# Ten of sixteen expert pairs: rows stored in DRAM and fetched per token, in place of the scatter matmul

## The chip, the cores and the metric

The kernel runs on one core of a Trainium2 chip. The time is device microseconds (us) of one launch. A NeuronCore has five engines with their own instruction queues: TensorE (PE, matmuls; its weight loads are listed apart as PEld), VectorE (DVE), ScalarE (ACT), GpSimd (POOL) and SyncE (SP, which here issues nearly all DMAs). They meet only through semaphores. Data lie in DRAM, in SBUF (128 partitions) and in PSUM, the matmul's output banks.

## The reference

Two layers of a streaming encoder on 512 tokens of width 1024 in float32. Each layer mixes tokens, attends to a memory, and ends with a mixture of experts, which is what the change touches:

```
for l in range(DEPTH):                    # 2 layers
    ...mixers, cross-attention, layer norms...
    g_p, g_idx   = top_1(softmax(t @ w_group))              # 4 groups
    e_p, e_idx   = top_2(softmax(logits of the 8 experts of that group))
    gate[t, e]   = g_p * e_p / sum(e_p)                     # 2 of 32 experts a token
    for e in range(32):
        h   = silu(t @ w_gate[e]) * (t @ w_up[e])           # 1024 -> 256
        out = out + (h @ w_down[e]) * gate[:, e]            # 256 -> 1024
    x = layer_norm(ALPHA * x + out)
```

An expert's weights are 1024x512 (gate and up) and 256x1024 (down) floats, 3.1 MB; 32 experts are 100.7 MB a layer.

## The kernel before, in words

Each expert has 64 slots; a token chosen by more than 64 goes to an overflow loop that runs after the experts. A token's slot number is 64 e + its rank in expert e, kept for its two experts in `s` (tokens on partitions, four tiles of 128 tokens). Two experts with neighbouring numbers form a pair of 128 slots, so a layer has 16 pairs; pairs 2q and 2q+1 share a block of 256 slots whose tokens are gathered by one-hot matmuls (`gather`, L1313) into a transposed tile `XX`.

The loop of `moe` (L1421) makes one run per pair p. On PE a run is, in this order: `down` of pair p-1 (h @ w_down, L1383, two halves of 512 columns), `up` of pair p (L1360, 8 steps of contraction for 2 experts), then four gather chunks for the next block (L1320) with `turn` of pair p (two transposes of h, L1373) and, between them, the scatter of pair p-1. `scatter` (L1497) multiplies a one-hot matrix `ohT` (128 slots by 512 tokens) with the pair's output `y`, for four token tiles and two halves: 8 results, each of 2 matmuls, because `y` is held as a rounded part and a rest (`e_y`, L1385 on ACT and L1386 on DVE, both with the gate `ws` as factor). Each result is added to the residual `x` on DVE (L1506). `onehot_rows` (L1476) makes `ohT` and `ws` with five DVE passes over 512 columns a pair. The last two blocks' runs (14 and 15) gather nothing. After run 15 `down` and the scatter of pair 15 follow, with sums for the layer norm (L1508).

Weights come in tiles of 128x1024 floats (512 KB): 8 for gate and up and 4 for down, 12 a pair, 192 a layer. `moe_raw` (L369) hands out buffers for them from a ring of 22: five `e2`, four `e1`, three each of `raw`, `whi`, `wlo`, and one 4-fold buffer `T16` (printed T). SP issues the loads in the ring's order, and waits in its queue until a buffer's last reader is done. A load of SP also waits until the one that used its completion semaphore is done; there are eight of these, so about eight loads are under way at a time. In the last run of layer 0 `fill_ahead` (L1391) loads two tiles of the memory (`in_memT`) for the next layer into one `whi` and one `wlo`, which ACT and DVE then split into a rounded part and a rest (L350, L351).

The order on each queue is that of a scheduler in the tile framework, which places instructions by their own due times; `issue_after` (`chain`, L279) keeps the PE runs of the loop in the order above.

Of the kernel before, what the change touches and what calls it, by code (L numbers as in the profile page):

```python
# [8 lines left out]
F32 = mybir.dt.float32  # L9
# [12 lines left out]
P = 128  # L22
# [186 lines left out]
class K:  # L209
    def __init__(self, ctx, tc, a):  # L210
        self.tc, self.nc, self.a = tc, tc.nc, a
        self.n = 0
        self.n_e1, self.n_e2, self.n_raw = 8, 5, 0
        self.n_rw, self.n_hi, self.n_lo, self.n_fw = 3, 3, 3, 3
        self.fills = [dict(f) for f in FILLS]
        self.mark, self.marks = None, False
        self.n_gap, self.n_u1, self.n_u2, self.n_qk = 1, 12, 8, 2
        self.paged = {}
# [150 lines left out]
    def moe_raw(self):  # L369
# [970 lines left out]

    def experts(self, Xs, gu, dn, ws, page, dpage=None):

# [34 lines left out]
        def down(hf, run):  # L1377
            if hf == 0:
                y.extend(self.t([P, D], "e_y", 2, F32R, self.mp) for _ in range(2))
            po, c = self.bank(self.pj), slice(hf * 512, (hf + 1) * 512)  # L1380
            for k in range(2):
                for i in range(n):
                    run.append(nc.tensor.matmul(po[CAP * i:CAP * i + CAP, :], st["hT"][:, k, CAP * i:CAP * i + CAP],  # L1383
                                                st["w"][k][i][:, c], start=k == 0, stop=k == 1))
            nc.scalar.activation(y[0][0:R, c], po[0:R, :], AF.Copy, scale=ws)  # L1385
            nc.vector.scalar_tensor_tensor(y[1][0:R, c], po[0:R, :], ws, y[0][0:R, c], op0=OP.mult, op1=OP.subtract)  # L1386
# [22 lines left out]
    def moe(self, l, r, X, x, following):  # L1409
# [9 lines left out]
        last = NE // 2 - 1  # L1419
        self.marks, before = True, None  # L1420
        for p in range(NE // 2):  # L1421
            q, pr = p // 2, p % 2
            e = 2 * p
            if p == last:
                self.fill = iter(())
                if following and self.n_gap:
                    self.fill_ahead(following)
            up, act, turn, down, y = self.experts(
                XX[:, q % 2, :, 128 * pr:128 * pr + 128], [a["gu"][l * NE + e + i] for i in range(2)],
                [a["dn"][l * NE + e + i] for i in range(2)], ws[:, p:p + 1], self.moe_raw,  # L1430
                None if p < last else lambda: self.t([P, 1024], "e2", self.n_e2, pool=self.e2))

# [205 lines left out]
    def layer(self, l, x_src, xT):  # L1638
# [89 lines left out]
```

## Time and profile before

| | |
|---|---|
| median of 3 runs | 1618.11 us (1613.19 to 1619.2) |
| the profiled execution | 1623.95 us, its span 1622.1 us |
| PE, DVE, ACT, POOL busy | 96%, 66%, 36%, 2% of the span |
| mean granted TensorE clock | 0.978 of full speed |
| DMA in all | 303.04 MB, 186 GB/s over the span |
| experts of layer 0: first `up` to the last scatter | 497.88 to 792.2 us |
| experts of layer 1: first `up` to the last scatter | 1289.04 to 1581.6 us |

Busy time of PE is that of modelled, overlapping matmuls, so a busy PE need not be at its peak. DMA share is the mean busy share of the 16 DMA engines. A row of the waits says which engine and line waited and what came last before it went on. The two layers' expert stages are alike: the second starts 791.2 us after the first, and takes 1.7 us less from its first `up` to its last scatter.

### The profile page before, as it was taken

What the parts mean: (1) busy time and instruction counts of PE and PEld (TensorE: products, weight loads), DVE (VectorE), ACT (ScalarE), POOL (GpSimd) and SP (SyncE); (2) the same over time, 40 slices, a digit from 0 to 9 for tenths busy, and PEclk for the clock granted to TensorE, in tenths of its full rate; (3) what the DMA queues carried; (4) which work ended last, traced back from release to release, by engine and by line L of the source; (5) the groups of instructions that cost most, each with busy time, mean ns of one, the idle gap of its engine ahead of it and who ended that gap; (6) DMA issues with size and microseconds to landing.
All of it is one profiled execution on the core that took longest, in us unless ns stands there. A gap on an engine that the chain in (4) does not pass through costs nothing. (4 is left out here: it accounts for less than half of the span.)

```text
span 1622.1 us, 25953 instructions
## 1 busy us (share of the span) xinstructions
PE 1555.0 (96%) x10270; PEld 1151.0 (71%) x10270; DVE 1067.8 (66%) x2352; ACT 575.9 (36%) x1026; POOL 32.5 (2%) x44
## 2 busy tenths in 40 slices
PE   7999999999999999999889999999999999999994
PEld 6988876898896555555579888669889855555542
DVE  6768678675568954445767857777655798545454
ACT  6434346324323222222463442552342332222212
POOL 0000000010000000000000000001000000000100
PEclk9999899999999999999999989999999999999997
DMA  6432220522437999996543332033224599899861
GB/s 218 149 119 80 79 72 20 177 68 82 155 121 268 381 341 343 342 352 247 212 152 106 104 98 93 6 122 94 92 86 153 184 351 373 326 339 346 333 238 53
DMA packets 90656, 303.04 MB, mean 187 GB/s; under 512 B 10404, under 2 KB 10916, under 8 KB 90404
## 3 DMA queue, kind: packets, MB, share of 16 engines
q1 hardware_dynamic: 90532, 301.36, 52.7%
q8 instruction: 81, 1.33, 0.3%
q14 instruction: 43, 0.35, 0.1%
HBM read 292.93 MB, written 8.39 MB: 186 GB/s over the span
## 5 line engine op out<-in xcount | busy, mean ns | idle before, releaser
L386 PE MATMUL pj<-whi,T 128*128 128x256 f32 x640 | 183.4, 287 | 4.5 <-ACT T L846 2.8
L1506 DVE TENSOR_TENSOR e<-e,sm 128x512 f32<-128x512 f32 x240 | 153.2, 683 | 51.1 <-PE sm L1502 50.7
L388 PE MATMUL pj<-wlo,T 128*128 128x256 f32 x640 | 182.9, 286 | 3.8 <-DVE wlo L351 3.8
L387 PE MATMUL pj<-whi,T 128*128 128x256 f32 x640 | 182.4, 285 | 0.0
L386 PE MATMUL pj<-T,whi 128*128 128x512 f32 (+1 forms) x368 | 135.3, 368 | 5.9 <-ACT T L350 5.6
L1502 PE MATMUL sm<-e_y,e_oT 128*128 128x512 f32 x512 | 139.3, 397 | 1.3 <-ACT e_y L1385 0.8
L351 DVE TENSOR_TENSOR wlo<-raw,whi 128x1024 fp32r<-128x1024 f32 x86 | 104.7, 1221 | 51.2 <-ACT whi L350 50.7
L387 PE MATMUL pj<-T,wlo 128*128 128x512 f32 (+1 forms) x368 | 135.9, 370 | 2.3 <-DVE wlo L351 2.3
L1320 PEld LDWEIGHTS sm<-oh,T 128*128 128x128 f32 x896 | 117.5, 188 | 25.7 <-issue 17.8
L388 PE MATMUL pj<-T,whi 128*128 128x512 f32 (+1 forms) x368 | 135.0, 368 | 0.0
L1320 PE MATMUL sm<-oh,T 128*128 128x256 f32 x896 | 129.6, 287 | 0.0
L386 PEld LDWEIGHTS pj<-whi,T 128*128 128x128 f32 x640 | 123.9, 194 | 5.8 <-ACT T L846 3.0
L388 PEld LDWEIGHTS pj<-wlo,T 128*128 128x128 f32 x640 | 123.8, 194 | 5.3 <-DVE wlo L351 5.1
L350 ACT CAST whi<-raw 128x1024 fp32r<-128x1024 f32 x86 | 89.8, 1048 | 105.2 <-PE pj L387 57.4
L387 PEld LDWEIGHTS pj<-whi,T 128*128 128x128 f32 x640 | 123.9, 194 | 0.2
L1360 PE MATMUL pj<-e,T 128*64 128x512 f32 x448 | 110.2, 593 | 0.0
L1310 ACT ACTIVATE T<-sm,vec 128x256 f32<-128x256 f32 x116 | 65.3, 566 | 105.1 <-PE sm L1320 105.1
L1502 PEld LDWEIGHTS sm<-e_y,e_oT 128*128 128x128 f32 x512 | 88.1, 188 | 20.4 <-ACT e_y L1385 3.3
L1368 DVE TENSOR_TENSOR e_sl<-e_sl,pj 128x256 f32<-128x256 f32 x32 | 13.5, 421 | 132.7 <-ACT e_sl L1367 132.6
L1385 ACT ACTIVATE e_y<-pj,rws 128x512 fp32r<-128x512 f32 x64 | 43.8, 687 | 118.6 <-PE pj L1383 106.7
L1360 PEld LDWEIGHTS pj<-e,T 128*64 128x64 f32 x448 | 35.1, 137 | 69.9 <-issue 67.7
L386 PEld LDWEIGHTS pj<-T,whi 128*128 128x128 f32 x368 | 70.5, 192 | 17.5 <-ACT T L350 6.4
(483 smaller groups left out, 3200.0 us busy)
## 6 DMA issues: line engine op xcount, KB each, us to landing
e<-in_gu SPq DMA_DIRECT2D x112, 512.0 KB, 9.3
raw<-in_pieces SPq DMA_DIRECT2D x94, 512.0 KB, 3.6
e<-in_dn SPq DMA_DIRECT2D x60, 512.0 KB, 7.6
T<-in_gu SPq DMA_DIRECT2D x44, 512.0 KB, 7.4
wlo<-in_gu SPq DMA_DIRECT2D x36, 512.0 KB, 8.9
whi<-in_gu SPq DMA_DIRECT2D x34, 512.0 KB, 8.8
raw<-in_gu SPq DMA_DIRECT2D x34, 512.0 KB, 8.5
fw<-in_pieces SPq DMA_DIRECT2D x60, 256.0 KB, 3.0
```

Of the source, the lines that this page charges most:

```text
L350: self.nc.scalar.copy(hi, src)
L351: self.nc.vector.tensor_tensor(lo, src, hi, op=OP.subtract)
L386: mm(ps, a[0], b[0], start=first, stop=False)
L387: mm(ps, a[1], b[0], start=False, stop=False)
L388: return mm(ps, a[0], b[1], start=False, stop=last)
L1310: self.nc.scalar.activation(Xs[:, f, :], ps, AF.Identity, scale=v[:, VC_LG + f:VC_LG + f + 1], bias=v[:, VC_LB + f:VC_LB + f + 1])
L1320: run.append(nc.tensor.matmul(ps, X[i][t][:, f * P:(f + 1) * P], oh[:, t, :], start=i + t == 0, stop=i + t == NT))
L1360: run.append(nc.tensor.matmul(st["h"][CAP * i:CAP * i + CAP, :], Xs[:, k, i * CAP:(i + 1) * CAP], st["w"][i][:, (k % 2) * 512:(k % 2 + 1) ...
L1368: nc.vector.tensor_tensor(sl[0:R], sl[0:R], st["h"][0:R, DE:], op=OP.mult)
L1385: nc.scalar.activation(y[0][0:R, c], po[0:R, :], AF.Copy, scale=ws)
L1502: m = nc.tensor.matmul(ps, ohT[:, t * P:(t + 1) * P], y[i][0:n, c], start=i == 0, stop=i == 1)
L1506: nc.vector.tensor_tensor(x[t][:, c], x[t][:, c], ps, op=OP.add)
```

## The change

Pairs 0 to 9 no longer have a one-hot matrix, a scatter or additions. Their `down` copies each PSUM half unscaled into one float32 tile `e_y` (half 0 by ACT, half 1 by DVE), and ACT issues a DMA that stores its 128 rows at slots 128 p to 128 p + 127 of a DRAM tensor `yd`, one for each layer. At the start of run 12 `stored_rows` is recorded: for each of a token's two experts and each token tile, GpSimd clears a buffer of the ring, then issues an indirect DMA that fetches, by slot number (`si`, an integer copy of `s`), each token's row of `yd`; slots of 1280 and above are out of bounds and fetch nothing. DVE multiplies the fetched tile by the token's gate and adds it to `x`. That is 8 tiles of 128x1024 a layer. Pairs 10 to 15 keep the scatter. Since the 8 fetched tiles come from the ring, the pairs after them use other buffers than before; in the last pair the `T16` part of the ring is skipped.

```
--- before.py
+++ after.py
@@ -215,6 +215,7 @@
         self.fills = [dict(f) for f in FILLS]
         self.mark, self.marks = None, False
         self.n_gap, self.n_u1, self.n_u2, self.n_qk = 1, 12, 8, 2
+        self.n_st = 10
         self.paged = {}
         pool = lambda name, bufs=1, **k: ctx.enter_context(tc.tile_pool(name=name, bufs=bufs, **k))
         self.cp = pool("cp")
@@ -372,6 +373,9 @@
         ring += [("raw", self.n_rw, self.wp)] * self.n_rw + [("whi", self.n_hi, self.wp)] * self.n_hi
         ring += [("wlo", self.n_lo, self.wp)] * self.n_lo
         i = self.n_raw % (len(ring) + 4)
+        if i == len(ring) and self.tail:
+            self.n_raw += 4
+            i = 0
         self.n_raw += 1
         if i < len(ring):
             tag, n, pool = ring[i]
@@ -1338,7 +1342,7 @@
                 nc.scalar.activation(Xs[:, f, :], ps[:, k * CAP:(k + 1) * CAP], AF.Identity,
                                      scale=v[:, VC_LG + f:VC_LG + f + 1], bias=v[:, VC_LB + f:VC_LB + f + 1])
 
-    def experts(self, Xs, gu, dn, ws, page, dpage=None):
+    def experts(self, Xs, gu, dn, ws, page, dpage=None, dst=None):
 
 
         nc = self.nc
@@ -1376,12 +1380,17 @@
 
         def down(hf, run):
             if hf == 0:
-                y.extend(self.t([P, D], "e_y", 2, F32R, self.mp) for _ in range(2))
+                y.extend(self.t([P, D], "e_y", 2, F32R if dst is None else F32, self.mp) for _ in range(2 if dst is None else 1))
             po, c = self.bank(self.pj), slice(hf * 512, (hf + 1) * 512)
             for k in range(2):
                 for i in range(n):
                     run.append(nc.tensor.matmul(po[CAP * i:CAP * i + CAP, :], st["hT"][:, k, CAP * i:CAP * i + CAP],
                                                 st["w"][k][i][:, c], start=k == 0, stop=k == 1))
+            if dst is not None:
+                self.copy(y[0][:, c], po, "ad"[hf])
+                if hf:
+                    nc.scalar.dma_start(dst, y[0])
+                return
             nc.scalar.activation(y[0][0:R, c], po[0:R, :], AF.Copy, scale=ws)
             nc.vector.scalar_tensor_tensor(y[1][0:R, c], po[0:R, :], ws, y[0][0:R, c], op0=OP.mult, op1=OP.subtract)
 
@@ -1418,17 +1427,23 @@
         ws = self.t([P, NE // 2], "rws")
         last = NE // 2 - 1
         self.marks, before = True, None
+        yd, si = self.yd[l], self.t([P, NT, 2], "rsi", dt=I32)
+        nc.vector.tensor_copy(si, s)
         for p in range(NE // 2):
+            if p == self.n_st + 2:
+                self.stored_rows(x, r["w"], yd, si)
             q, pr = p // 2, p % 2
             e = 2 * p
             if p == last:
+                self.tail = True
                 self.fill = iter(())
                 if following and self.n_gap:
                     self.fill_ahead(following)
             up, act, turn, down, y = self.experts(
                 XX[:, q % 2, :, 128 * pr:128 * pr + 128], [a["gu"][l * NE + e + i] for i in range(2)],
                 [a["dn"][l * NE + e + i] for i in range(2)], ws[:, p:p + 1], self.moe_raw,
-                None if p < last else lambda: self.t([P, 1024], "e2", self.n_e2, pool=self.e2))
+                None if p < last else lambda: self.t([P, 1024], "e2", self.n_e2, pool=self.e2),
+                yd[p * P:(p + 1) * P, :] if p < self.n_st else None)
 
             with self.run_of() as run:
                 if before:
@@ -1449,14 +1464,14 @@
                     ohs.append(self.slots_onehot(s, 256 * (q + 1), 256))
                 full = [lambda run, c=4 * pr + i, o=ohs[-1], X2=XX[:, (q + 1) % 2]: self.gather(l, X2, o, 256, X, (c,), run)
                         for i in range(4)]
-            ohT = self.onehot_rows(srow, p, ws)
+            ohT = self.onehot_rows(srow, p, ws) if p >= self.n_st else None
             with self.run_of() as run:
                 for i in range(4):
                     if i == 3:
                         turn(run)
                     for f in full[i:i + 1]:
                         f(run)
-                    if before:
+                    if before and before[2] is not None:
                         for t in (2 * i % NT, (2 * i + 1) % NT):
                             self.scatter(x, before[1], before[2], t, i // 2, run=run)
             before = down, y, ohT
@@ -1472,6 +1487,17 @@
                 self.scatter(x, y, ohT, t, hf, sums[:, t, hf:hf + 1])
         self.overflow(l, r, X, x, sums)
         return self.last_norm(x, gb, sums)
+
+    def stored_rows(self, x, w, yd, si):
+
+        nc = self.nc
+        for i in range(2):
+            for t in range(NT):
+                v = self.moe_raw()
+                nc.gpsimd.memset(v, 0.0)
+                nc.gpsimd.indirect_dma_start(v, None, yd, bass.IndirectOffsetOnAxis(ap=si[:, t, i:i + 1], axis=0),
+                                             bounds_check=self.n_st * P - 1, oob_is_err=False)
+                nc.vector.scalar_tensor_tensor(x[t], v, w[:, t, i:i + 1], x[t], op0=OP.mult, op1=OP.add)
 
     def onehot_rows(self, srow, p, ws):
 
@@ -1671,7 +1697,7 @@
         rt, self.sp = self.open("rt")
         mp, self.mp = self.open("mp")
         e2, self.e2 = self.open("e2")
-        self.n_raw = 0
+        self.n_raw, self.tail = 0, False
         r = self.router_state(l)
         X = r["X"]
         self.proj_residual(l, PI_XO, oT, x, None, lambda t, st, gb: self.router_tile(x[t], t, st, r),
@@ -1700,6 +1726,7 @@
         self.wps, self.wp = self.open("wp", side="right")
         self.xd = self.dp.tile([T, D], F32, name="xd")
         self.kvd = self.dp.tile([4, P, 1024], F32, name="kvd")
+        self.yd = [self.dp.tile([self.n_st * P, D], F32, name=f"yd{l}") for l in range(layers)]
         self.early = {PI_MISC: self.raw_piece(PI_MISC)}
         xT = self.load_xT()
         self.setup()
```

The diff moves lines below it by up to 26: L1360, L1383, L1502 and L1506 of before are L1364, L1387, L1528 and L1532 of the changed file.

PE, layer 0, the first rows after `up` in a run (run 6 of both); `oh` and T make a gather chunk, `e_y` and `e_oT` a scatter, `e_sl` is `turn`, `e_hT` the next `down`.

```order
L1320 MATMUL sm_1098_6200<-oh_1094_6183,T16_737_4360 128x256 x4
L1320 MATMUL sm_1098_6200<-oh_1094_6183,T16_738_4361 128x256 x4
L1502 MATMUL sm_1099_6210<-e_y_1075_6121,e_oT_1058_6036 128x512
L1502 MATMUL sm_1099_6210<-e_y_1076_6122,e_oT_1058_6036 128x512
L1502 MATMUL sm_1100_6214<-e_y_1075_6121,e_oT_1058_6036 128x512
L1502 MATMUL sm_1100_6214<-e_y_1076_6122,e_oT_1058_6036 128x512
L1320 MATMUL sm_1101_6218<-oh_1094_6183,T16_737_4360 128x256 x4
L1320 MATMUL sm_1101_6218<-oh_1094_6183,T16_738_4361 128x256 x4
L1502 MATMUL sm_1102_6228<-e_y_1075_6121,e_oT_1058_6036 128x512
L1502 MATMUL sm_1102_6228<-e_y_1076_6122,e_oT_1058_6036 128x512
```

```order
L1324 MATMUL sm_1032_5976<-oh_1031_5967,T16_737_4362 128x256 x4
L1324 MATMUL sm_1032_5976<-oh_1031_5967,T16_738_4363 128x256 x4
L1324 MATMUL sm_1033_5986<-oh_1031_5967,T16_737_4362 128x256 x4
L1324 MATMUL sm_1033_5986<-oh_1031_5967,T16_738_4363 128x256 x4
L1324 MATMUL sm_1034_5996<-oh_1031_5967,T16_737_4362 128x256 x4
L1324 MATMUL sm_1034_5996<-oh_1031_5967,T16_738_4363 128x256 x4
L1377 MATMUL sm_1035_6006<-const_98,e_sl_1029_5962 128x128 x2
L1324 MATMUL sm_1037_6011<-oh_1031_5967,T16_737_4362 128x256 x4
L1324 MATMUL sm_1037_6011<-oh_1031_5967,T16_738_4363 128x256 x4
L1387 MATMUL pj_1039_6022<-whi_1025_5954,e_hT_1036_6009 64x512
```

Before, each gather chunk is followed by four scatter matmuls; in the changed kernel the four chunks stand together with `turn`, and the next run's `down` follows them.

DVE, layer 0, the end of run 11: before, the eight additions of pair 10's scatter and then the evictions of pair 11 (`e_y`); `e1` is `x`.

```order
L1506 TENSOR_TENSOR e1_530_3054<-e1_530_3054,sm_1241_6843 128x512
L1506 TENSOR_TENSOR e1_531_3055<-e1_531_3055,sm_1245_6862 128x512
L1506 TENSOR_TENSOR e1_532_3056<-e1_532_3056,sm_1246_6866 128x512
L1484 TENSOR_SCALAR e_oT_1265_6930<-e_s_873_5240,const_96 128x512
L1485 SCALAR_TENSOR_TENSOR e_oT_1265_6930<-e_s_875_5247,const_96,e_oT_1265_6930 128x512
L1386 SCALAR_TENSOR_TENSOR e_y_1248_6871<-pj_1249_6872,rws_857_5190,e_y_1247_6870 128x512
L1386 SCALAR_TENSOR_TENSOR e_y_1248_6871<-pj_1250_6879,rws_857_5190,e_y_1247_6870 128x512
L1368 TENSOR_TENSOR e_sl_1264_6927<-e_sl_1264_6927,pj_1251_6886 128x256
```

```order
L1532 TENSOR_TENSOR e1_530_3056<-e1_530_3056,sm_1157_6572 128x512
L1500 SCALAR_TENSOR_TENSOR e1_529_3055<-whi_1163_6599,rw_877_5253,e1_529_3055 128x1024
L1532 TENSOR_TENSOR e1_531_3057<-e1_531_3057,sm_1161_6591 128x512
L1532 TENSOR_TENSOR e1_532_3058<-e1_532_3058,sm_1162_6595 128x512
L1500 SCALAR_TENSOR_TENSOR e1_530_3056<-whi_1164_6605,rw_877_5253,e1_530_3056 128x1024
L1500 SCALAR_TENSOR_TENSOR e1_531_3057<-whi_1165_6611,rw_877_5253,e1_531_3057 128x1024
L1500 SCALAR_TENSOR_TENSOR e1_532_3058<-wlo_1166_6617,rw_877_5253,e1_532_3058 128x1024
L1500 SCALAR_TENSOR_TENSOR e1_529_3055<-wlo_1167_6623,rw_877_5253,e1_529_3055 128x1024
L1500 SCALAR_TENSOR_TENSOR e1_530_3056<-wlo_1168_6629,rw_877_5253,e1_530_3056 128x1024
L1500 SCALAR_TENSOR_TENSOR e1_531_3057<-T16_1169_6635,rw_877_5253,e1_531_3057 128x1024
L1500 SCALAR_TENSOR_TENSOR e1_532_3058<-T16_1169_6635,rw_877_5253,e1_532_3058 128x1024
L1395 SCALAR_TENSOR_TENSOR e_y_1171_6647<-pj_1172_6648,rws_857_5192,e_y_1170_6646 128x512
```

The eight additions of fetched rows (L1500) stand between the sixth addition of pair 10's scatter and the evictions of pair 11 (L1395); each waits for its own indirect DMA.

SP, layer 0, the loads of pair 15 (8 of `in_gu`, 4 of `in_dn`) and the two of `in_memT`.

```order
L1058 DMA whi_1380_7416<-in_memT 128x1024
L1058 DMA wlo_1381_7420<-in_memT 128x1024
L1351 DMA e2_1387_7441<-in_gu 128x1024
L1351 DMA e1_1388_7443<-in_gu 128x1024
L1351 DMA e1_1389_7449<-in_gu 128x1024
L1351 DMA e1_1390_7451<-in_gu 128x1024
L1351 DMA e1_1391_7457<-in_gu 128x1024
L1351 DMA raw_1392_7459<-in_gu 128x1024
L1351 DMA raw_1393_7465<-in_gu 128x1024
L1351 DMA raw_1394_7467<-in_gu 128x1024
L1351 DMA e2_1395_7473<-in_dn 128x1024
L1351 DMA e2_1396_7475<-in_dn 128x1024
```

```order
L1062 DMA whi_1269_7048<-in_memT 128x1024
L1062 DMA wlo_1270_7052<-in_memT 128x1024
L1355 DMA whi_1276_7073<-in_gu 128x1024
L1355 DMA whi_1277_7075<-in_gu 128x1024
L1355 DMA whi_1278_7081<-in_gu 128x1024
L1355 DMA wlo_1279_7083<-in_gu 128x1024
L1355 DMA wlo_1280_7089<-in_gu 128x1024
L1355 DMA wlo_1281_7091<-in_gu 128x1024
L1355 DMA e2_1282_7097<-in_gu 128x1024
L1355 DMA e2_1283_7099<-in_gu 128x1024
L1355 DMA e2_1284_7105<-in_dn 128x1024
L1355 DMA e2_1285_7107<-in_dn 128x1024
```

Before, pair 15 is loaded into `e2`, `e1` and `raw`; in the changed kernel into the three `whi`, the three `wlo` and then `e2`. The third `whi` and the third `wlo` have first to be released by the splits of the two memory tiles.

## Rows read from the trace of the kernel before

**Rows 1.** The page, parts 1 and 2: engines, and GB/s in the span's 40 slices.

```profile
PE 1555.0 (96%) x10270; PEld 1151.0 (71%) x10270; DVE 1067.8 (66%) x2352; ACT 575.9 (36%) x1026; POOL 32.5 (2%) x44
...
GB/s 218 149 119 80 79 72 20 177 68 82 155 121 268 381 341 343 342 352 247 212 152 106 104 98 93 6 122 94 92 86 153 184 351 373 326 339 346 333 238 53
```

**Rows 2.** Timeline of PE: start, us, line, tiles, shape, count; idle before in brackets.

```profile
41.87 0.58 PE L386 MATMUL pj<-whi,T 128*128 128x256 f32 x1 [2.77 <-ACT T L846]
...
511.79 0.64 PE L1383 MATMUL pj<-e,e_hT 128*64 128x512 f32 x1 [1.25 <-ACT e_hT L1375]
...
607.32 2.31 PE L1360 MATMUL pj<-e,T 128*64 128x512 f32 x9
...
615.34 1.09 PE L1502 MATMUL sm<-e_y,e_oT 128*128 128x512 f32 x4
616.26 1.12 PE L1320 MATMUL sm<-oh,T 128*128 128x256 f32 x8
...
625.72 0.60 PE L1360 MATMUL pj<-T,T 128*64 128x512 f32 x2
...
781.09 2.79 PE L1383 MATMUL pj<-e,e_hT 128*64 128x512 f32 x10
```

**Rows 3.** Waits of SP's own queue, 540 to 755 us: total, times, longest.

```profile
SPq L1351 <- PE pj L1383: 87.7, 13, 11.1
SPq L1351 <- PE pj L1360: 28.0, 33, 2.6
```

**Rows 4.** Stretches: us; busy PE, PEld, DVE, ACT, POOL; PEclk, DMA share, GB/s.

```profile
40.00:45.00 5.00, 2.34 (x9) 2.05 (x10) 4.94 (x6) 1.80 (x4) 0.00 (x0) 0.67 0.29 88
45.00:50.00 5.00, 5.00 (x31) 5.00 (x31) 4.85 (x7) 2.47 (x3) 0.00 (x0) 0.65 0.78 247
...
420.00:525.00 105.00, 102.29 (x765) 86.07 (x764) 70.39 (x226) 33.24 (x49) 2.19 (x4) 1.00 0.56 187
510.00:515.00 5.00, 3.75 (x21) 1.54 (x21) 3.96 (x5) 1.78 (x3) 0.00 (x0) 1.00 1.01 363
525.00:555.00 30.00, 30.00 (x161) 16.82 (x162) 29.15 (x73) 7.83 (x14) 0.00 (x0) 1.00 1.01 385
525.00:750.00 225.00, 225.00 (x1205) 127.08 (x1205) 133.31 (x271) 54.16 (x99) 0.00 (x0) 1.00 0.92 344
607.30:625.70 18.40, 18.40 (x100) 10.28 (x98) 9.71 (x19) 4.39 (x8) 0.00 (x0) 1.00 0.91 343
...
1315.00:1360.00 45.00, 45.00 (x246) 26.52 (x246) 43.67 (x110) 10.92 (x21) 0.00 (x0) 1.00 1.01 390
...
1615.00:1620.00 5.00, 0.00 (x0) 0.00 (x0) 2.59 (x4) 0.00 (x0) 1.06 (x2) 0.50 0.65 241
```

**Rows 5.** Timeline of SP's queue, end of layer 0's experts.

```profile
737.38 2.20 SPq L1351 DMA_DIRECT2D e<-in_dn  x4
754.78 0.33 SPq L1058 DMA_DIRECT2D whi<-in_memT  x1
...
768.90 1.75 SPq L1351 DMA_DIRECT2D e<-in_dn  x4
```

**Rows 6.** The page, part 6: DMA issues, count, size, us to landing.

```profile
e<-in_dn SPq DMA_DIRECT2D x60, 512.0 KB, 7.6
...
xd<-T SPq DMA_DIRECT2D x8, 256.0 KB, 2.5
```

**Rows 7.** Lines, 520 to 860 us: busy us, mean ns of one, idle before.

```profile
L1506 DVE TENSOR_TENSOR e<-e,sm 128x512 f32<-128x512 f32 x120 | 76.6, 683 | 25.6 <-PE sm L1502 25.4
L1386 DVE SCALAR_TENSOR_TENSOR e_y<-pj,rws,e_y 128x512 fp32r<-128x512 f32 x32 | 23.9, 749 | 13.3 <-ACT e_y L1385 13.0
...
L1605 DVE SCALAR_TENSOR_TENSOR T<-T,lst,e 128x1024 f32<-128x1024 f32 x4 | 5.0, 1281 | 0.8 <-POOL lst L1604 0.8
...
L865 POOL MEMSET T<- 128x1024 f32 x1 | 1.0, 952 | 6.2 <-DVE T L351 6.2
```

More of the change, by code (lines that the diff above doesn't have):

```diff
@@ L217, in __init__ @@
         self.n_gap, self.n_u1, self.n_u2, self.n_qk = 1, 12, 8, 2
+        self.n_st = 10
         self.paged = {}
@@ L374, in moe_raw @@
         i = self.n_raw % (len(ring) + 4)
+        if i == len(ring) and self.tail:
+            self.n_raw += 4
+            i = 0
         self.n_raw += 1
@@ L1339, in gather_few, with experts @@
                                      scale=v[:, VC_LG + f:VC_LG + f + 1], bias=v[:, VC_LB + f:VC_LB + f + 1])
-    def experts(self, Xs, gu, dn, ws, page, dpage=None):
+    def experts(self, Xs, gu, dn, ws, page, dpage=None, dst=None):
         nc = self.nc
@@ L1378, in down @@
             if hf == 0:
-                y.extend(self.t([P, D], "e_y", 2, F32R, self.mp) for _ in range(2))
+                y.extend(self.t([P, D], "e_y", 2, F32R if dst is None else F32, self.mp) for _ in range(2 if dst is None else 1))
             po, c = self.bank(self.pj), slice(hf * 512, (hf + 1) * 512)
@@ L1384, in down @@
                                                 st["w"][k][i][:, c], start=k == 0, stop=k == 1))
+            if dst is not None:
+                self.copy(y[0][:, c], po, "ad"[hf])
+                if hf:
+                    nc.scalar.dma_start(dst, y[0])
+                return
             nc.scalar.activation(y[0][0:R, c], po[0:R, :], AF.Copy, scale=ws)
@@ L1420, in moe @@
         self.marks, before = True, None
+        yd, si = self.yd[l], self.t([P, NT, 2], "rsi", dt=I32)
+        nc.vector.tensor_copy(si, s)
         for p in range(NE // 2):
+            if p == self.n_st + 2:
+                self.stored_rows(x, r["w"], yd, si)
             q, pr = p // 2, p % 2
@@ L1424, in moe @@
             if p == last:
+                self.tail = True
                 self.fill = iter(())
@@ L1430, in moe @@
                 [a["dn"][l * NE + e + i] for i in range(2)], ws[:, p:p + 1], self.moe_raw,
-                None if p < last else lambda: self.t([P, 1024], "e2", self.n_e2, pool=self.e2))
+                None if p < last else lambda: self.t([P, 1024], "e2", self.n_e2, pool=self.e2),
+                yd[p * P:(p + 1) * P, :] if p < self.n_st else None)
             with self.run_of() as run:
@@ L1451, in moe @@
                         for i in range(4)]
-            ohT = self.onehot_rows(srow, p, ws)
+            ohT = self.onehot_rows(srow, p, ws) if p >= self.n_st else None
             with self.run_of() as run:
@@ L1458, in moe @@
                         f(run)
-                    if before:
+                    if before and before[2] is not None:
                         for t in (2 * i % NT, (2 * i + 1) % NT):
@@ L1474, in moe, with stored_rows @@
         return self.last_norm(x, gb, sums)
+    def stored_rows(self, x, w, yd, si):
+        nc = self.nc
+        for i in range(2):
+            for t in range(NT):
+                v = self.moe_raw()
+                nc.gpsimd.memset(v, 0.0)
+                nc.gpsimd.indirect_dma_start(v, None, yd, bass.IndirectOffsetOnAxis(ap=si[:, t, i:i + 1], axis=0),
+                                             bounds_check=self.n_st * P - 1, oob_is_err=False)
+                nc.vector.scalar_tensor_tensor(x[t], v, w[:, t, i:i + 1], x[t], op0=OP.mult, op1=OP.add)
     def onehot_rows(self, srow, p, ws):
@@ L1673, in layer @@
         e2, self.e2 = self.open("e2")
-        self.n_raw = 0
+        self.n_raw, self.tail = 0, False
         r = self.router_state(l)
@@ L1702, in run @@
         self.kvd = self.dp.tile([4, P, 1024], F32, name="kvd")
+        self.yd = [self.dp.tile([self.n_st * P, D], F32, name=f"yd{l}") for l in range(layers)]
         self.early = {PI_MISC: self.raw_piece(PI_MISC)}
```

## The prediction

> **What bounds the kernel now.** I read the page first: PE is busy 96% of the span, and DMA is low except in two long plateaus at 326 to 381 GB/s, the expert stages of the two layers [rows 1]. The change touches only these; the instructions outside them stand in the same order as before. Next the timeline of PE in one run: from the `up` of run 6 at 607.32 to that of run 7 at 625.72 is 18.40 us [rows 2], with PE busy for all of it [rows 4]. Next, who holds whom: SP's queue, between 540 and 755 us, waited 87.7 + 28.0 us for PE to release weight buffers [rows 3]. So PE sets the pace and the loads follow it. But they follow closely: one run moves 12 x 0.524 = 6.29 MB in 18.40 us, 343 GB/s at a DMA share of 0.91 [rows 4]. Where the loads run without being held, at the start of each stage, the share is 1.01 and the rate 385 GB/s over 30 us and 390 GB/s over 45 us [rows 4]. I take 388 GB/s as what the 16 engines give. The reader should see two limits 12% apart: a run cannot become shorter than its transfers.
>
> **The change part by part, for one layer.**
>
> *Scatter matmuls removed.* Runs 1 to 10 lose four groups of four matmuls. One group takes 616.26 - 615.34 = 0.92 us [rows 2], four 3.7 us, so a run of PE alone is 18.4 - 3.7 = 14.7 us and ten save 37 us. This is the upper bound of the gain; both layers would give 74 us.
>
> *Transfers added.* Ten stores of 512 KB (5.24 MB) and eight fetches. The inputs of the reference send 650 (layer 0) and 674 (layer 1) of the 1024 token-expert choices to the first twenty experts within their 64 slots, so 2.7 MB of rows of 4 KB are fetched. A run of the first ten then moves 6.81 MB, which at 388 GB/s takes 17.6 us. That is over PE's 14.7 and only 0.8 under the present 18.4. The bytes, not the matmuls, now set the end, and the sum goes by them. The nearest row for a store is the end of the kernel, where only stores run: 241 GB/s at share 0.65, so 371 at a full share [rows 4], within 5% of a load. I count a store as a load. Its bounds are nothing, if stores fill time in which loads wait, and 2 x 2.5 = 5.0 us each, from the 256 KB stores of `xd` one at a time [rows 6].
>
> *The sum by bytes.* From 420 to 525 us 105 x 187 = 19.6 MB moved [rows 4]; less 2.3 MB that are not expert weights, 33 of the 192 loads are in by 525. Until then nothing much changes, since the buffers were filled beforehand. To come are 159 loads (83.4 MB), 5.2 MB of stores, 2.7 MB of fetches and, in layer 0, two memory tiles (1.0 MB): 92.3 MB, or 91.3 in layer 1. At 388 GB/s that is 238 and 235 us, so the last load is in at 763 and at the place of 760 in layer 1. Before, the last four loads were issued at 768.90 [rows 5] and the last `down` began at 781.09 [rows 2]. It is this `down` that needs them. Without gaps it could come 18 and 21 us earlier, where PE alone would allow 37.
>
> *What the DMA loses again.* (a) The eight fetch buffers leave 14 of 22 for weights around run 12, and the loads of pair 13 wait until DVE has read the fetched tiles, eight passes like L1605, 8 x 1.28 = 10.2 us [rows 7], in one piece before the evictions of pair 11. Those evictions hide behind the `up` of run 12, and 14 buffers are still 1.2 pairs; I put 5 us of gaps on each layer, between none and the 10.2 us. (b) In layer 0 the loads of pair 15 from the third `whi` on wait for the memory split, which stands behind the eviction of `down` in run 15. Before, the memory tiles went out at 754.78, a run ahead [rows 5], and pair 15 used other buffers. By the durations that is an idle PE of 3 to 4 us in run 15. After an idle time of 2.77 us PE ran at half clock in the trace: clock 0.67 and 0.65 in the next two stretches of 5 us [rows 2, 4]. After 1.25 us of idle the clock stayed at 1.00 [rows 2, 4]. So (b) costs up to 7 us, of which 2 lie under the 5 of (a), since the bytes catch up while PE waits.
>
> *Everything else.* DVE loses 80 additions (80 x 0.683 = 55 us), 20 passes like L1386 (15 us) and ten pairs' one-hot passes, and gains 10 copies and the 10.2 us; it was never the bound. ACT issues a store once DVE's copy of half 1 is done, under 1 us in a queue with half its time free. POOL clears eight tiles, 8 x 0.952 = 7.6 us [rows 7], in an otherwise empty queue. The semaphore order lets a load stand behind a store at some places of SP's queue; the store is due three loads ahead, and landing takes 7.6 us for 512 KB under load [rows 6], so I count nothing; if this cover went, it would be 1 or 2 us a pair.
>
> *Indirect DMAs.* The trace has none. From below they cost nothing beyond their bytes, and no less, since nothing else goes away with them. From above: the first can go when pair 9's store has landed, in run 10, and DVE needs them at the end of run 11, some 25 us later; eight in a row have to take under 3 to 4 us each to be free, and each us above that holds DVE, then PE, for up to 8 us a layer. The nearest row, a 512 KB load under load, lands in 7.6 us but with eight under way at a time [rows 6]. I take them as hidden.
>
> So layer 0 gains 18 - 5 - 2 = 11 us and layer 1 gains 21 - 5 = 16, about 26 together with rounding. The profiled execution took 1623.95 us and would take 1598. The median of the runs is 5.8 us below that execution, so the forecast for the median is 1618.1 - 26 = 1592 us.
>
> The Trainium skill has a rule against the 388: "DMA: Bandwidth & Descriptors", Specifications, puts the HBM limit of one core at about 358 GB/s. By that figure 92.3 MB would take 258 us, the last load would be in at 783, and the change would lose some 6 us a layer with its gaps. Its section on bandwidth says that this is with the other core of the pair streaming too; the 385 and 390 of the trace agree with that reading.
>
> **The rivals.**
>
> *The mixed stream is slower than pure loads.* Stores and scattered rows between loads may keep the engines from 388. For it speaks that the 225 us from 525 on held only 344 [rows 4]; against it that SP was held by PE for half of that time [rows 3]. At 360 GB/s the 92 MB take 256 us, the last load is in at 781, and with the gaps the last `down` begins 5 to 7 us later than now: 1630 us. At 344 it would be 1650.
>
> *The fetches come late (slower).* Place: the eight L1500 at the end of run 11, in DVE's queue ahead of pair 11's evictions. Late fetches stop DVE, then PE's scatter of pair 11, then the loads of pair 13 that need the same buffers, so PE and DMA stand together. Price: each us over 3 to 4 us per fetch costs 8 us a layer. At 7 us each it is 24 to 32 us a layer against a gain of 13: about 1645. It decides from 5 us each. Nothing in the profile speaks for or against, as no indirect DMA is in it.
> The Trainium skill, "SBUF — State Buffer", in "SBUF: two separate sides", gives a reason: while DVE runs certain SBUF-to-SBUF passes, GpSimd cannot write its descriptors. No run here shows it yet.
>
> *PE falls to half clock.* With transfers as the bound PE waits about 3 us in a run of 17.6, in three or four pieces of about 1 us. If these count like the 2.77 us above, each run has some 6 us at half clock and takes 3 us more, 17.7 us and its waits: as long as now. Against it: 1.25 us did nothing. Then 1614, no change.
>
> *The transfers go faster.* At 405 GB/s without gaps the last load is in at 753: 28 us a layer, 1564.
>
> **How the numbers follow.** The forecast has 50% (its own range 1574 to 1607), faster transfers 10%, half clock 14%, a slower mixed stream 15%, late fetches 11%. The range 1567 to 1638 leaves out about 1 in 10 on each side. A difference under 0.5% (8 us) cannot be told from none here. Faster is the forecast's 49%, the faster transfers' 10% and 1% of the rest: 0.60. No change is the half clock's 12% and a few per cent from the edge of the mixed stream and the forecast: 0.16. The rest, 0.24, is slower.
>
> **What would show it.** Right: runs 4 to 10 of 17 to 18 us with DMA share at 1.0, PE idle in pieces of about 1 us before L1364 that wait for DMA; SP's waits for PE in the plateau down from 116 us to under 30; the last `down` of layer 0 at 768 to 772; about 4 us of idle PE in run 15 of layer 0 but not of layer 1. Wrong: runs 1 to 10 near 14.7 us, which would mean more than 388 GB/s; a share of 1.0 with a rate below 370; DVE waiting at L1500 for the fetches for more than a few us; a granted clock under 0.95 in runs 4 to 10.

## The result

The changed kernel takes 1596.24 us (median of 6 runs, 1593.44 to 1604.94), the kernel before 1614.9 us (6 runs, 1613.19 to 1619.2). The ratio is 0.9891, with a 95% interval of 0.9863 to 0.9918: 17.6 us faster by the ratio, 18.7 by the medians. The forecast was 1592 us and 26 us faster.

The profiled executions are 1623.95 - 1596.71 = 27.2 us apart, which looks like the forecast, but 5.3 us of it lie outside the stages that the change touches. The first `up` of layer 0 comes at 493.87 instead of 497.88, behind code that the change does not touch; in the profiles of the eleven experiments below it comes at 490.3 to 496.3. And from the last `down` of layer 0 to the first `up` of layer 1 another 1.3 us went, in a stretch that takes 501.7 to 508.0 us in the thirteen profiles. From the first `up` to the last `down` layer 0 takes 276.6 us instead of 283.2, layer 1 267.6 instead of 283.0: **6.6 and 15.3 us**, together 22, where 11 and 16 were forecast.

The page after, parts 1 and 2, answers to [rows 1]: PE lost 51 us of work, slices of the two plateaus reach 408 to 411 GB/s where 381 was the most.

```profile
PE 1503.8 (94%) x9950; PEld 1094.2 (69%) x9950; DVE 919.4 (58%) x2050; ACT 557.7 (35%) x1006; POOL 67.5 (4%) x76
...
GB/s 222 147 126 86 75 72 21 173 66 93 137 113 261 411 358 389 387 408 282 227 175 93 116 103 89 27 79 140 80 93 163 159 305 378 398 388 399 409 297 53
```

The timeline of PE in layer 0 after the change, which answers to [rows 2] (start, us, line, tiles, shape, count; idle before in brackets): the beginnings of runs 4, 5 and 10, run 11 with the beginning of run 12, and run 15.

```profile
555.52 4.03 PE L1364 MATMUL pj<-e,T 128*64 128x512 f32 x17
...
570.18 1.89 PE L1364 MATMUL pj<-wlo,T 128*64 128x512 f32 x8
...
656.77 1.89 PE L1364 MATMUL pj<-raw,T 128*64 128x512 f32 x8
...
664.83 1.93 PE L1364 MATMUL pj<-wlo,T 128*64 128x512 f32 x6 [1.08 <-DMA wlo<-in_gu]
...
674.39 1.96 PE L1364 MATMUL pj<-e,T 128*64 128x512 f32 x8
...
678.67 2.85 PE L1364 MATMUL pj<-e,T 128*64 128x512 f32 x8 [1.08 <-DMA e<-in_gu]
682.39 1.93 PE L1364 MATMUL pj<-e,T 128*64 128x512 f32 x6 [0.87 <-DMA e<-in_gu]
...
686.92 1.93 PE L1364 MATMUL pj<-e,T 128*64 128x512 f32 x6 [1.06 <-DMA e<-in_gu]
...
700.19 1.89 PE L1364 MATMUL pj<-T,T 128*64 128x512 f32 x8
...
751.99 1.89 PE L1364 MATMUL pj<-whi,T 128*64 128x512 f32 x8
757.23 1.56 PE L1364 MATMUL pj<-whi,T 128*64 128x512 f32 x2 [3.36 <-DMA whi<-in_gu]
...
770.43 2.79 PE L1387 MATMUL pj<-e,e_hT 128*64 128x512 f32 x10
```

Read the starts of the runs one after the other. Run 4 takes 570.18 - 555.52 = 14.66 us, and so do runs 1 to 3: the scatter is gone and nothing takes its place. Runs 6 to 10 take 89.3 us together (87.6 in layer 1), 17.9 each, with waits for weights. Run 11, which scatters again, takes 700.19 - 674.39 = 25.8 us instead of 18.4, with a wait before nearly every pair of weight tiles. Runs 12 and 13 are at 18.4 as before. Run 15 has one long wait, of 3.36 us.

The stretches after (columns as in [rows 4]):

```profile
525.00:555.00 30.00, 30.00 (x170) 15.07 (x168) 7.63 (x23) 7.30 (x15) 0.00 (x0) 1.00 1.03 411
555.00:585.00 30.00, 30.00 (x167) 15.51 (x165) 5.21 (x14) 6.98 (x14) 0.00 (x0) 1.00 0.95 354
585.00:690.00 105.00, 95.38 (x454) 43.17 (x451) 12.95 (x29) 18.62 (x37) 15.59 (x16) 1.00 1.01 389
690.00:735.00 45.00, 45.00 (x247) 26.86 (x247) 31.20 (x44) 11.41 (x21) 0.00 (x0) 1.00 1.03 409
...
755.00:760.00 5.00, 2.77 (x6) 0.71 (x7) 0.19 (x1) 0.00 (x0) 0.00 (x0) 0.77 0.94 347
760.00:765.00 5.00, 4.79 (x19) 1.44 (x17) 0.00 (x0) 0.00 (x0) 0.00 (x0) 0.89 1.03 415
```

And the waits of SP's own queue from 540 to 755 us, which answer to [rows 3]. Those for PE fell from 115.7 to 9.3 us, as forecast. At the top stands a wait that the forecast had counted at nothing: loads that wait for a store of `yd`.

```profile
SPq L1355 <- DMA yd<-e_y: 51.4, 8, 8.5
SPq L1355 <- DMA e<-in_gu: 27.6, 25, 2.1
SPq L1355 <- DVE T L352: 12.3, 1, 12.3
...
SPq L1355 <- PE pj L1387: 5.7, 13, 1.9
SPq L1355 <- PE pj L1364: 3.6, 12, 0.4
```

Not every such wait costs transfers. From 525 to 555 us SP waited 8.2 us for stores in two waits, the longer of 4.8, and the rate was still 411 GB/s; from 555 to 585 it waited 14.4 us in two, the longer of 8.5, and the rate fell to 354.

### The profile page after: what moved, and what is told of

Same layout as the page of the kernel before. It is cut to its first block, busy times and chain, and to the rows that moved or that the text cites. A ratio compares the mean times of both kernels' runs of the same rounds, so it can differ in the third digit from the quotient of the medians.

```text
span 1594.9 us, 25206 instructions
## 1 busy us (share of the span) xinstructions
PE 1503.8 (94%) x9950; PEld 1094.2 (69%) x9950; DVE 919.4 (58%) x2050; ACT 557.7 (35%) x1006; POOL 67.5 (4%) x76
## 3 DMA queue, kind: packets, MB, share of 16 engines
q0 software_dynamic: 2304, 5.43, 0.9%
## 5 line engine op out<-in xcount | busy, mean ns | idle before, releaser
L1364 PE MATMUL pj<-e,T 128*64 128x512 f32 x480 | 128.7, 597 | 11.9 <-DMA e<-in_gu 11.9
L1324 PEld LDWEIGHTS sm<-oh,T 128*128 128x128 f32 x896 | 111.3, 188 | 22.4 <-issue 19.5
L1324 PE MATMUL sm<-oh,T 128*128 128x256 f32 x896 | 122.1, 287 | 0.0
L1371 ACT ACTIVATE e_sl<-pj 128x256 f32<-128x256 f32 x32 | 12.3, 384 | 279.9 <-PE pj L1364 279.9
L1364 PEld LDWEIGHTS pj<-e,T 128*64 128x64 f32 x480 | 39.1, 136 | 94.4 <-issue 57.5
L390 PEld LDWEIGHTS pj<-T,whi 128*128 128x128 f32 x368 | 70.4, 192 | 17.1 <-ACT T L351 6.1
L391 PEld LDWEIGHTS pj<-T,wlo 128*128 128x128 f32 x368 | 70.6, 192 | 13.5 <-DVE wlo L352 2.9
L392 PEld LDWEIGHTS pj<-T,whi 128*128 128x128 f32 x368 | 70.4, 192 | 11.4 <-issue 1.1
L351 ACT CAST fwh<-fw 128x512 fp32r<-128x512 f32 x60 | 37.2, 620 | 82.0 <-PE fb L391 27.0
```

Source lines behind the costliest of these rows:

```text
L351: self.nc.scalar.copy(hi, src)
L390: mm(ps, a[0], b[0], start=first, stop=False)
L391: mm(ps, a[1], b[0], start=False, stop=False)
L392: return mm(ps, a[0], b[1], start=False, stop=last)
L1324: run.append(nc.tensor.matmul(ps, X[i][t][:, f * P:(f + 1) * P], oh[:, t, :], start=i + t == 0, stop=i + t == NT))
L1364: run.append(nc.tensor.matmul(st["h"][CAP * i:CAP * i + CAP, :], Xs[:, k, i * CAP:(i + 1) * CAP], st["w"][i][:, (k % 2) * 512:(k % 2 + 1) ...
```

## The experiments

Theory after reading this trace: PE gains 3.75 us in each of runs 1 to 10; from run 6 on the transfers take most of it back, and the fetches take 7 to 8 us in run 11. Rivals: it is not bytes but the order of SP's queue and the turn of the buffers; or the costs are the same wherever and however many the pairs are. "Stage" below is the time from the first `up` to the last `down`, layer 0 and layer 1.

**before_again.** The kernel before, unchanged.

> The kernel before, once more, with a profile. In the changed kernel loads that nothing holds ran at 409 GB/s (690 to 735 us), in the profiled execution of before at 385 to 390. If the faster rate belongs to the changed program, the first 30 us after 525 show 385 to 390 GB/s again and no 15 us stretch over 395; if it belonged to that execution or chip, they show 400 or more. Run period 18.4 us in runs 1 to 13 by either.

1615.54 us, a single run. Runs 1 to 13 take 18.4 us, the stages 283.2 and 282.7, and from 525 to 555 the rate is 381 GB/s:

```profile
525.00:555.00 30.00, 30.00 (x158) 15.33 (x154) 29.23 (x80) 6.72 (x12) 0.00 (x0) 1.00 1.01 381
```

So the 409 belongs to the changed program.

**n5.**

```diff
-        self.n_st = 10
+        self.n_st = 5
```

> Five pairs are stored and fetched instead of ten. Theory (bytes): the gain of the change is made in runs 1 to 5, which PE does in 14.66 us from loads that came early, and runs 6 to 10 give nothing since DMA cannot bring 6.8 MB in 14.7 us. Then five pairs keep the whole gain of runs 1 to 5 (5 x 3.74 = 18.7 us a layer), runs 6 to 14 are at 18.4 with under 2 us of waits together, the fetch of half the rows costs no 7 us, and the idle of run 15 in layer 0 (7 us) stays: first up to last down 272 to 274 us in layer 0 and 264 to 266 in layer 1 (276.6 and 267.6 with ten), about 1589 us. Rival (each pair pays its 3.7 us wherever it is, and tail and fetch cost the same whatever the number): half the pairs, half the gain, about 1605 us.

Ratio 0.9862 (0.9838 to 0.9886), 1594.78 us: the same as with ten pairs. Stages 277.0 and 268.9, where I expected 273 and 265. Runs 1 to 4 keep the whole gain and run 5 keeps it in layer 1 (16.8 us in layer 0), runs 7 to 14 have no waits, and run 6 takes 21.9 and 22.9 us. Of the two, the theory is nearer: half the pairs did not mean half the gain. But I had run 6 wrong, and put it on the fetches.

**nobytes.**

```diff
-                                             bounds_check=self.n_st * P - 1, oob_is_err=False)
+                                             bounds_check=0, oob_is_err=False)
```

> The eight fetches are issued, waited for and added as in the changed kernel, into the same buffers, but the bound on the row index is 0, so that nearly no row is transferred (the part of the first ten pairs is left out of the output). Theory (bytes): the 7.4 and 8.1 us that run 11 takes over 18.4 are the 2.7 MB of the rows at 389 to 409 GB/s (6.6 to 6.9 us), so run 11 falls to 18.4 to 20 us, 13 us in the two layers: about 1583 us. Rival (buffers and latency): the eight buffers that the fetches hold and the order of POOL, store, fetch and DVE make the wait; then run 11 stays at 24 to 26 us and the time at 1594 to 1597.

Run 11 takes 21.6 and 20.5 us (25.8 and 26.5 with the rows): 4.2 and 6.0 of the 7.4 and 8.1 us are the rows' bytes, and 2 to 3 us stay, so neither expectation holds in full. Whose these 2 to 3 us are is not shown: the buffers and the order are as before, but SP also waited 7.2 us for a store just ahead of run 11's loads (655 to 700 us). The time, 1618.47 us, can't be compared: with a part of layer 0's output missing layer 1 routes otherwise, and its overflow loop runs twice, as this row of its `e_sl` shows (one run of the loop, 33.5 us, from 1555.2 to 1588.7; in the changed kernel the count is 1).

```profile
L1588 DVE TENSOR_TENSOR e_sl<-e_sl,pj x2: 423/423/423, 1555.2 to 1588.7; 64x256 f32<-64x256 f32 x2
```

Less that it is 1585, against 1583 expected.

**noscat.**

```diff
-                if hf:
-                    nc.scalar.dma_start(dst, y[0])
...
-            if p == self.n_st + 2:
-                self.stored_rows(x, r["w"], yd, si)
```

> The scatter of the first ten pairs is left out and neither stored nor fetched (their part of the output is left out): PE's relief alone, with the loads of before. Theory (bytes): runs 6 to 10 take the 6.29 MB of a run at 400 to 409 GB/s, 15.4 to 15.7 us, and no run 11 of 25 us; first up to last down 247 to 251 us in both layers, 1615 - 2 x 34 = 1543 to 1552 us in all. Rival (SP's order and the turn of the buffers, not bytes, hold PE in runs 6 to 10): these stay at 17 us or more, 1560 or more in all.

Runs 1 to 10 all take 14.66 us, the stages 244.8 and 246.1: PE never waits. The loads run at one rate:

```profile
525.00:555.00 30.00, 30.00 (x170) 15.14 (x168) 7.65 (x22) 7.48 (x15) 0.00 (x0) 1.00 1.03 410
585.00:690.00 105.00, 105.00 (x584) 55.39 (x581) 24.67 (x48) 25.03 (x49) 0.00 (x0) 1.00 1.03 409
```

Its 1577.26 us contain the same second overflow loop (1514.3 to 1549.6, 35.3 us); less that 1542. So 409 GB/s is what the engines give to loads alone, and stores and fetches together cost 32 and 22 us a layer, 7 of layer 0's in run 15.

**poolst.** The trace after shows loads that wait for stores; this takes away what makes them wait.

```diff
-                    nc.scalar.dma_start(dst, y[0])
+                    nc.gpsimd.dma_start(dst, y[0])
```

> The changed kernel, with its ten stores issued from POOL's queue instead of ACT's; they then count on other semaphores and no load on SP waits for a store. In the changed kernel SP waited 32.2 us for stores in the 105 us from 585 to 690, at 389 GB/s; where no store was in the way loads ran at 409. Theory (the shared semaphores cost the 5%): SP's waits for stores go, the rate of runs 6 to 10 is 405 to 410, five runs take 83 to 85 us instead of 89.3 and 87.6, about 1586 us. Rival (stores between loads are slower whatever queue they are in): the rate stays at 385 to 395, the five runs at 87 to 90 us, 1594 to 1598 us.

Ratio 0.9776 (0.9744 to 0.9809), 1581.24 us, 15 us under the changed kernel. The five runs take 81.2 and 81.0 us, less than the 83 to 85 expected. SP no longer waits for any store, and the same mixture of loads, stores and fetches runs at 409:

```profile
585.00:690.00 105.00, 98.59 (x502) 48.83 (x499) 19.15 (x42) 21.51 (x43) 18.14 (x21) 1.00 1.03 409
```

A share of 1.01 with 389 GB/s, as in the changed kernel, was therefore not a full DMA. The edit changes two things, the semaphore that a store counts on and the DMA queue that carries it (q10, `hardware_dynamic`, becomes q0, `software_dynamic`), and no run separates them. For the semaphore speak SP's waits for stores, which are gone, and the time from a store's issue to its landing, which hardly changes (median 7.3 us in the changed kernel, 7.1 here).

**late.**

```diff
             if p == last:
...
-                if following and self.n_gap:
-                    self.fill_ahead(following)
...
                     up(k, run)
+                    if p == last and k == KC - 2 and following and self.n_gap:
+                        self.fill_ahead(following)
```

> The changed kernel, but the loads and splits of the memory tiles for the next layer are issued after the weights of up of pair 15, so that these no longer wait for the split. Theory: the 3.4 us of idle PE and the half clock behind it in run 15 of layer 0 go, from the first up of pair 15 to the last down 11.5 us instead of 18.4, layer 1 unchanged: about 1589 us. Rival: the memory tiles come some 20 us later and the work on them, which fills PE behind the experts, is late instead; the idle time moves behind the last down and the time stays at 1594 to 1598.

From the first `up` of pair 15 to the last `down` it is now 12.5 us instead of 18.4, without a wait for weights:

```profile
753.74 2.31 PE L1364 MATMUL pj<-whi,T 128*64 128x512 f32 x9
756.75 2.31 PE L1364 MATMUL pj<-wlo,T 128*64 128x512 f32 x9
758.89 1.89 PE L1364 MATMUL pj<-e,T 128*64 128x512 f32 x8
760.71 3.03 PE L1528 MATMUL sm<-e_y,e_oT 128*128 128x512 f32 x12
...
766.26 1.07 PE L1387 MATMUL pj<-e,e_hT 128*64 128x512 f32 x2
```

The way from there to layer 1 is 506.3 us, as in the changed kernel (506.6), so nothing is given back. The total does not show it: ratio 0.9858 (0.9822 to 0.9894), 1594.8 us, where the changed kernel's six runs lie between 1593.44 and 1604.94. The stages are 274.1 and 271.2 us: layer 1, which the edit does not touch, was 3.6 us longer in this execution, and layer 0 lost elsewhere 3.5 of the 5.9 us that it gained in run 15. The profiled execution lost 2.3 us in run 0, where PE had been idle for 1.96 us, and the granted clock was below full in two places:

```profile
505.00:510.00 5.00, 3.04 (x9) 0.92 (x10) 3.76 (x4) 2.24 (x4) 0.00 (x0) 0.75 0.95 354
...
685.00:690.00 5.00, 4.84 (x13) 1.22 (x10) 0.00 (x0) 0.00 (x0) 0.00 (x0) 0.66 1.03 404
```

The second place is run 11: waits of 1.34, 0.96 and 1.05 us stood before it, and the run took 26.8 us instead of 25.8. By itself this run leaves the 6 us open; poollate, below, decides.

**n5spread.** Beside `n_st = 5`:

```diff
-            if p == self.n_st + 2:
-                self.stored_rows(x, r["w"], yd, si)
+            if 0 <= p - self.n_st - 2 < 8:
+                self.stored_rows(x, r["w"], yd, si, (p - self.n_st - 2,))
```

(`stored_rows` now takes the numbers of the fetches to issue.)

> Five pairs stored, and the eight fetches issued one in each of runs 7 to 14 instead of all ahead of run 7. With five pairs and all fetches at once run 6 took 21.9 and 22.9 us, since they came when the loads' lead was used up, though DMA had share 0.85 to 0.97 from 690 on. Theory (bytes at the wrong place): run 6 at 18.4 to 19.5, the runs behind it at 18.4, 7 us less than with all at once, 1586 to 1589 us. Rival (a fetch costs by what it holds: its buffer and the order of SP's queue behind it): each of the eight runs loses 0.5 to 2 us and the time is 1594 or more.

Ratio 0.9827 (0.9799 to 0.9856), 1588.32 us, as much as expected, but not for that reason. The stages, 275.7 and 267.2, are only 1.3 and 1.7 us shorter than n5's, the rest of the 6.5 us between the medians lies outside them, and run 6 still takes 22.5 us in layer 0 and 20.6 in layer 1 (21.9 and 22.9 with all fetches at once), though at most one or two fetches fall there. The fetches behind it cost nothing (18.4 us in runs 7 to 13). So run 6 was not the fetches in the main. SP's waits from 555 to 600 us name a candidate:

```profile
SPq L1355 <- DMA yd<-e_y: 14.9, 2, 8.1
SPq L1355 <- DMA T<-in_gu: 5.7, 6, 1.3
```

**best5.** n5spread with the edits of poolst and late.

> The last three edits together: five pairs, fetches one a run, stores on POOL's queue, memory tiles after the weights of pair 15. If the costs are separate, as the theory has them, run 5 falls from 16.8 to 14.7 in layer 0, run 6 to 18.4, run 15 of layer 0 to 15 us, with no wait of over 1 us in runs 1 to 14: first up to last down 264 to 266 us in both layers, 1577 to 1581 us. If they cover each other, one remaining wait takes over and it stays above 1585.

Ratio 0.9786 (0.975 to 0.9822), 1580.77 us; stages 265.0 and 264.6; run 6 is at 18.41 in both layers and no run waits for a load. That settles run 6: with the stores moved to POOL's queue its loss is gone, in layer 1 too, where late's edit does nothing.

**best8, best10, poollate.** More pairs with these edits; `poollate` is the changed kernel with those of poolst and late alone, its fetches all at once.

```diff
-            if p == self.n_st + 2:
-                self.stored_rows(x, r["w"], yd, si)
+            n0, n1 = [8 * min(max(v - 12, 0), 4) // 4 for v in (p, p + 1)]
+            if n1 > n0:
+                self.stored_rows(x, r["w"], yd, si, range(n0, n1))
```

(This is best10's; best8 has 11 for the 12.)

> As best5, with eight pairs stored and the eight fetches two a run in runs 11 to 14. With the stores on POOL's queue the changed kernel did runs 1 to 6 in 14.66 us, 7 and 8 in 32.9 together, at 409 GB/s. Theory (bytes at 409): runs 1 to 8 lose only what DMA lacks, 3.6 to 4 us in runs 7 and 8, runs 9 to 14 stay at 18.4 since DMA needs 15.4 for the weights and 1 to 2 for the fetches; first up to last down 265 - 3 x 3.74 + 3.6 = 257.4 us in both layers, 1566 us. Rival (fetches hold buffers and DVE whenever they come): runs 11 to 13 at 20 us or more, 1572 to 1580 us.

> As best5, with ten pairs stored and the fetches two a run in runs 12 to 15. Theory (bytes at 409): runs 6 to 10 take 81 us as with stores on POOL's queue, the 7.3 us of run 11 are spread over runs 11 to 14, whose slack of 3 us each takes them up to about 2 us: first up to last down 265 - 18.7 + 7.8 + 2 = 256 us, 1563 us. Rival (the lead of the loads is used up by run 10 and the fetches come on top): runs 11 to 14 lose 6 us or more a layer, 1571 or more.

> The changed kernel with its stores on POOL's queue and the memory tiles after the weights of pair 15, all fetches at once as in the changed kernel. Theory: the two savings add up, run 15 of layer 0 takes 11.5 to 12.5 us up to its last down instead of 18.4, run 11 stays at 25 to 26: 1581 - 6 = 1575 us; best10 is 12 us faster, by its spread fetches alone. Rival: the saving in run 15 is given back behind the last down, 1579 to 1583 us.

best8: 0.9728 (0.9702 to 0.9754), 1570.62 us, stages 258.8 and 257.8; run 9 loses 1.0 to 1.2 us that I had not expected, but runs 11 to 13 stay at 18.4, so the rival falls. best10: **0.9686 (0.9666 to 0.9707), 1564.37 us**, the fastest, 32 us under the changed kernel; stages 257.4 and 256.1, near the 256 of the theory. poollate: 0.9718 (0.9703 to 0.9734), 1568.98 us. This is 12 us under poolst, of which late's edit alone can explain 6: the stage of layer 0 falls from 268.1 to 262.1, that of layer 1, which the edit does not touch, from 261.4 to 259.8, and the rest lies outside the stages (the first `up` comes 5.0 us earlier). Spreading the fetches is worth 4.6 us by the medians (4.8 and 3.7 us in the two stages), not the 12 expected. The timeline of best10's run 11:

```profile
665.73 1.90 PE L1364 MATMUL pj<-e,T 128*64 128x512 f32 x8
667.81 1.07 PE L1364 MATMUL pj<-e,T 128*64 128x512 f32 x2 [0.18 <-DMA e<-in_gu]
669.09 2.35 PE L1364 MATMUL pj<-e,T 128*64 128x512 f32 x8 [0.21 <-DMA e<-in_gu]
671.64 2.35 PE L1364 MATMUL pj<-e,T 128*64 128x512 f32 x8 [0.20 <-DMA e<-in_gu]
674.20 1.93 PE L1364 MATMUL pj<-e,T 128*64 128x512 f32 x6 [0.21 <-DMA e<-in_gu]
```

and its stretches:

```profile
585.00:690.00 105.00, 101.69 (x522) 50.74 (x520) 22.94 (x43) 22.63 (x44) 8.55 (x11) 1.00 1.03 410
690.00:735.00 45.00, 44.87 (x234) 24.55 (x231) 24.07 (x36) 9.54 (x18) 9.61 (x10) 1.00 1.03 408
```

The wait before a pair of tiles is 0.2 us where it was up to 1.1, and run 11 takes 21.7 us instead of 25.8. That is still 3.3 us over 18.4, though SP waits for no store and all but three of layer 0's eight fetches come later. But runs 7 to 10 take 16.0 + 17.1 + 16.1 + 16.7 us, as long as in poolst.

## Why the prediction was right, and where it was not

- **The direction and its reason hold.** PE's scatter goes (14.66 us a run, 14.7 forecast), and transfers, not PE, set what is left of the gain: without stores and fetches it is 38.4 and 36.9 us in the two layers (noscat), with them 6.6 and 15.3.
- **388 GB/s as the limit: wrong.** It is 409 (noscat, poolst). I called the loads of before in [rows 4] unheld without looking at SP's waits in that stretch; the waits that I read began at 540. From 525 to 555 SP had waited 12.2 of 30 us for PE (and from 1315 to 1360, the other stretch, 15.4 of 45):

```profile
SPq L1351 <- PE pj L1383: 12.2, 2, 6.1
SPq L1351 <- DMA T<-in_gu: 3.4, 4, 1.3
```

- **The semaphore order "counts nothing": wrong, and the largest error.** The text gave its price if the cover went as 1 or 2 us a pair; it is 8.1 and 6.5 us for the five runs 6 to 10 (poolst), 1.5 us a pair. That this error and the last cancelled is luck: 388 for loads and stores alike is nearly the 389 that a held SP made of the 409.
- **The place of the bound: wrong.** I took the sum of bytes up to the last load and expected runs 4 to 10 at 17 to 18 us. Runs 4 and 5 took 14.7 and 14.9 on the loads' lead, runs 6 to 10 17.9. What sets the end is the sum at run 11: by the end of its `up` 140 loads are needed, 107 of them after 525, 56.1 MB, with 5.2 MB of stores and 2.7 of fetches 64.0 MB. On the same count from the same distance to the first `up`, 521 here, to the last tiles at 686.92 that is 386 GB/s; the trace has 64.2 MB in that stretch, 387. Behind run 11 nothing waits for bytes; runs 12 to 14 are PE's 18.39, 18.41 and 15.00 us, and the DMA's spare 409 GB/s comes too late.
- **Fetches hidden, with 5 us of gaps: too low.** Run 11 costs 7.4 and 8.1 us. The fetched rows were in time: each landed in 9.0 to 10.8 us, POOL issued one in 1.0 us, and DVE did not wait before L1500; 4.2 and 6.0 us of the price are their bytes, in the run in which the lead was used up (nobytes); the cause of the rest stays open. The mechanism that I gave for the 5 us, loads of pair 13 that wait until DVE has read the fetched tiles, cost nothing that shows: runs 12 and 13 are at 18.4. The rival of late fetches falls, and so does the case that the rule of the Trainium skill, "SBUF — State Buffer", in "SBUF: two separate sides", would have made of it: POOL's fetches were issued at 666 to 681 us, where DVE was nearly idle, and best10, with five of its eight fetches where DVE is busy for 24 of 45 us, is the fastest, although DVE waits there once a layer for a fetch, 3.4 us. That does not test the rule itself.
- **The memory split in run 15 of layer 0: right.** 3 to 4 us idle and half clock behind it, up to 7 in all; measured 3.36 us, a granted clock of 0.77 and 0.89 in the next stretches (a mean of the two levels, 1.2 and 2.4 GHz), 6.9 us in all, none in layer 1. The sum has it wrong all the same: the text lets 2 of the 7 lie under the 5 of the gaps, which leaves 5 to take off, but "18 - 5 - 2" takes off 2. By its own words layer 0 would gain 8 us, 3 less, and the forecast be 1595. Nothing of the 6.9 was hidden.
- **How the errors add up.** Against the sum, layer 0 lost 4.9 us in run 15 and 2.4 in run 11, but runs 1 to 10 gained 21.2 us where 18 were forecast, and 0.3 went in run 0: 6.6 instead of 11. In layer 1 runs 1 to 10 gained 23.2 where 21 were forecast and run 11 cost 3.1 more than the 5, so its 15.3 lie near the 16 by two errors that cancel. The last `down` of layer 0 at 770.43, inside the forecast 768 to 772, is luck as well: the first `up` came 4.0 us early.
- **PE at half clock in runs 4 to 10: no.** Waits of 0.3 to 1.1 us left the clock at 1.00. It is not far off, though: in run 11 of late, waits of 1.34, 0.96 and 1.05 us came before a granted clock of 0.66, between the two levels.
- **The slower mixed stream: no** as a rate of the engines (409 in poolst), but the 354 to 389 GB/s of the changed kernel was what SP's waits for stores made of it. The 358 GB/s of the Trainium skill, "DMA: Bandwidth & Descriptors", Specifications, is passed by 51 in these traces with one core at work.

Why 22 us in the stages and 17.6 by the runs: the profiled execution of before was 9 us over the median of its runs. Against before_again, which lies at its median, the spans differ by 1613.7 - 1594.9 = 18.8 us: 6.6 + 15.1 in the stages, less 2.1 for a first `up` that comes later (493.87 against 491.74) and 0.7 between the layers and at the end. To set one execution against one other costs some 5 us either way here; the stages of before agree to 0.3 us.

## What to carry to other kernels

A sum of bytes has to be taken at every run of the loop, not only at its end: the place where the lead of the loads is used up sets the time, and spare bandwidth behind it buys nothing. A rate can be called a limit only where the issuing queue waited for nothing but its own transfers; look at the queue's waits of that same stretch. A new DMA on another queue can still hold the loads through a completion semaphore that they share: issue it where it counts on others, and see in the queue's waits that its name is gone. Here that was worth 15 us of 1596, the queue's kind changing with it.

## Not expected of the hardware

- A mean DMA share of 1.01 can hide 5% of lost rate: 389 GB/s at 1.01, 409 at 1.03, 381 at 1.01 in before_again.
- Loads, stores and indirect fetches together ran as fast as loads alone, 409 and 409 GB/s, with DVE busy for 18% and 23% of the time.
- A fetch by 128 row numbers, of which some 83 rows of 4 KB were moved (5.43 MB in 16 fetches), landed in 9.0 to 10.8 us in the changed kernel, as long as a load of `in_dn` there (median 10.0). With nearly no rows to move it took 6.4 to 7.8 us (nobytes).
- After an idle time of 1.96 us (late) PE's granted clock was 0.75 in that stretch; before, 1.25 us had left it at 1.00 and 2.77 had not. Three waits of 1.34, 0.96 and 1.05 us came before a stretch at 0.66 (late).
